# Expert gates of the first 128 tokens: from one-hot products on TensorE to indexed stores into a table in HBM

## The chip, the cores and the metric

The kernel runs on one core of a Trainium2 chip. The metric is the device time of one execution in microseconds (us). The engines are named as in the profile: PE is TensorE's matmuls, PEld its weight loads, DVE is VectorE, ACT is ScalarE, POOL is GpSimd, SP is SyncE, which issues the DMAs of the kernel before.

## What is computed

Two transformer blocks over 256 tokens. The change lies in the feed-forward layer of the first one, a retrieval over 16,384 single-neuron experts. Each of 8 heads picks 16 experts of a token by two half keys, and the gates are a softmax over the picked scores. Cut to what matters:

```python
def peer_ffn(n, w_q, sub_keys, expert_u, expert_v):
    q = (t @ w_q).reshape(T, 8, 2, 128)
    s = jnp.einsum('thsd,hskd->thsk', q, sub_keys)
    v_half, i_half = lax.top_k(s, 16)
    cand = (v_half[:, :, 0, :, None] + v_half[:, :, 1, None, :]).reshape(T, 8, 256)
    best, pos = lax.top_k(cand, 16)
    i1 = jnp.take_along_axis(i_half[:, :, 0], pos // 16, axis=-1)
    i2 = jnp.take_along_axis(i_half[:, :, 1], pos % 16, axis=-1)
    experts = (i1 * 128 + i2).reshape(T, 128)
    gates = jax.nn.softmax(best, axis=-1).reshape(T, 128)
    act = jax.nn.gelu(jnp.einsum('td,tkd->tk', x, expert_u[experts])) * gates
    return jnp.einsum('tk,tkd->td', act, expert_v[experts])
```

Two heads may pick the same expert for a token; their gates then add up.

## The kernel before, in words

The kernel does not gather experts. It computes the activations of all 16,384 experts for all 256 tokens, multiplies them with a dense matrix of gates that is zero where an expert was not picked, and multiplies the result with all of `expert_v`. Every weight comes in chunks of 512 KB. SP loads a chunk into `raw` (`pump_dma`, L345, four buffers), ACT copies it into a rounded high part `wh` and DVE subtracts to get the low part `wl` (`pump_split`, L352, three buffers of each), and PE multiplies with three products per pair of parts.

The stages around the change stand in this order. The mixer reads 45 chunks of `w_in` (L949). Then come 16 of `w_out`, 16 of `w_q`, which give the scores, then 128 chunks of `expert_u` (the loop at L1223, two chunks for each `j2`), which I call the U stage, and 128 chunks of `expert_v`, the V stage. A U chunk is 24 matmuls of 128x256 (`wa`, L436); chunk j holds the 128 experts with i2 = j, the partition is i1. Its result of two chunks lies in one PSUM bank `acc`, and `u_post` (L1206) puts the gelu of it into `hact`, a table in SBUF of 128 partitions x 128 chunks x 256 tokens (tiles `hactA`, `hactB`). In the V stage `w_split` (L1237) splits two chunks of `hact` into `wth` (ACT) and `wtl` (DVE), and `v_mm` multiplies.

Beside the chunks run side jobs: Python generators that are advanced by so many units after each chunk (`tick`, L412), which sets where their instructions stand in the program. A scheduler then places the instructions of all engines; each engine runs its own in order. `peer_side` (L1163) is the side job of the gates. For each block `tb` of 128 tokens, `topk1` picks 16 of each half, `topk2` combines them and ends with `isel` (minus i1, and i2) and the gates `gt`. PE transposes these into `idxT`. `g_side` (L1111) then takes four tokens at a time, which I call a quartet: ACT makes a one-hot matrix of i1 in `oA` (four instructions and one more over all four), DVE makes one of i2 scaled by the gates in `oB` (four instructions), and PE multiplies them into a bank `sm`, the dense gates of the token:

```python
act(oA[:, j], iota, AF.Square, bias=idxT[:, 0, t:t + 1])
ts(oB[:, j], iota, idxT[:, 1, t:t + 1], idxT[:, 2, t:t + 1], OP.is_equal, OP.mult)
...
mm(pg[:, j], A_[:, j], B_[:, j], True, True)
```

DVE multiplies the gates into those chunks of `hact` that are there already; ACT copies the gates of the later chunks into `hact`, where `u_post` multiplies the gelu onto them. In the kernel before, the first block's quartets are given out in turn with the selection of the second block (`alternate`, L1149), and the second block's quartets come after both.

Of the kernel before, what the change touches and what calls it, by code (L numbers as in the profile page):

```python
# [38 lines left out]
def _consts():  # L39
    cols, off = [], 0  # L40

    def put(name, arr):
        nonlocal off
        arr = np.asarray(arr, np.float32).reshape(128, -1)
        _C[name] = (off, arr.shape[1])
        cols.append(arr)
        off += arr.shape[1]

    i = np.arange(128)
    put("ident", np.eye(128))  # L50
    put("iota", np.broadcast_to(i[None, :], (128, 128)))
    first = off
# [155 lines left out]
def build(tc, a, out):  # L208
    nc = tc.nc
    top = ExitStack()  # L210
    with top:
# [53 lines left out]

        V, S, PE, SP = nc.vector, nc.scalar, nc.tensor, nc.sync

        def mm(o, l, r, start, stop_):
            PE.matmul(o, l, r, start=start, stop=stop_)  # L269

        def bank(tag):
            return ps.tile([128, 512], F, name=tag, tag=tag, bufs=4 if tag == "acc" else 2)
# [68 lines left out]
        st = {"n": 0, "dma": 0, "split": 0, "done": 0}  # L341
        RAW, SA, HB = 4, 2, 3
        raws, hs, ls, spare = {}, {}, {}, {}

# [390 lines left out]

        B0, B1 = slice(T0, T0 + 128), slice(T0 + 128, T0 + 256)

        def ssd_group(g):
            cc = slice(g * 384, (g + 1) * 384)
            hh = slice(6 * g, 6 * g + 6)  # L740
# [179 lines left out]
        def sc_chunks(i):  # L920
# [23 lines left out]
            post(1, fn)  # L944
            post(2, lambda ac=ac, i=i: tt(mixl[:, 12 + i], ac, mixh[:, 12 + i].bitcast(F), OP.subtract))

        z_chunk()
        si = 0
        for what in MIX[1:]:  # L949
# [52 lines left out]
        idxT = tp.tile([128, 3, 256], F, name="idxT")  # L1002
        ust = {"J": 0, "T": 0, "sc": set(), "topk": -1}

        scores = Pool(112, 128).tile([128, 32, 128], F, name="scores")

# [39 lines left out]
        def topk2(tb):  # L1046
# [18 lines left out]
                    top16(best[:, h], pos[:, h], cd[:, h, :50], w[:, :50], part)  # L1065
                yield 0.7

            gt = tp.tile([128, 8, 16], F, name="gt")
# [19 lines left out]
            tt(gt, gt, gs_[:, :, None].to_broadcast([128, 8, 16]), OP.mult)  # L1088
            yield
            isel = ih.bitcast(F).rearrange("p (s h) r -> p s h r", s=2)  # L1090
            for s in range(2):
                for h2 in range(4):
                    eq = gp.tile([128, 8, 64], F, name="cdw", bufs=1)
                    eq = eq.rearrange("p h c -> p (h c)").rearrange("p (h k r) -> p h k r", h=2, k=16)
                    hh = slice(2 * h2, 2 * h2 + 2)
                    tt(eq, iota[:, None, None, :16].to_broadcast([128, 2, 16, 16]),
                       pf[:, s, hh, :, None].to_broadcast([128, 2, 16, 16]), OP.is_equal)
                    yield 0.6
                    tt(eq, eq, ir[:, hh, s, None, :].to_broadcast([128, 2, 16, 16]), OP.mult)
                    yield 0.6  # L1100

                    V.tensor_reduce(out=isel[:, s, hh], in_=eq, op=OP.add, axis=AX.X, negate=(s == 0))
                    yield 0.6
            pt = bank("tr")
            for j, src in enumerate((isel[:, 0], isel[:, 1], gt)):
                PE.transpose(pt[:, j * 128:(j + 1) * 128], src.rearrange("p h r -> p (h r)"), ident)
            yield
            V.tensor_copy(idxT[:, :, tb * 128:(tb + 1) * 128],  # L1108
                          pt[:, :384].rearrange("p (j t) -> p j t", j=3))

        def g_side(tb):  # L1111
            ab, pm = None, None
            for t4 in range(tb * 32, tb * 32 + 34):
                if pm is not None:
                    q4, pg = pm
                    J = ust["J"]
                    tsl = (q4 * 4, q4 * 4 + 4)
                    for jj, _, hv_ in Hact(0, J, *tsl):
                        hv_ = hv_.rearrange("p j t -> p t j")
                        tt(hv_, pg[:, :, jj], hv_, OP.mult)  # L1120
                    ust["T"] = q4 * 4 + 4
                    late = (pg, J, tsl)
                    pm = None
                else:
                    late = None
                if ab is not None:
                    q4, A_, B_ = ab
                    pg = bank("sm").rearrange("p (t j) -> p t j", t=4)
                    for j in range(4):
                        mm(pg[:, j], A_[:, j], B_[:, j], True, True)  # L1130
                    pm = (q4, pg)
                    ab = None
                if t4 < tb * 32 + 32:
                    oA = gp.tile([128, 4, 128], F, name="oA", bufs=2)
                    oB = gp.tile([128, 4, 128], F, name="oB", bufs=2)

                    for j in range(4):
                        t = t4 * 4 + j
                        act(oA[:, j], iota, AF.Square, bias=idxT[:, 0, t:t + 1])
# [9 lines left out]
        def alternate(g1, g2):  # L1149
            gens = [g1, g2]  # L1150
            while gens:
                for g in list(gens):
                    try:
                        c = next(g)
                        yield c
                    except StopIteration:
                        gens.remove(g)
# [5 lines left out]
        def peer_side():  # L1163
            yield from paced(topk1(0), 1.3)
            yield from paced(topk2(0), 1.3)

            def second():
                yield from topk1(1)
                yield from topk2(1)

            yield from paced(alternate(g_side(0), second()), 1.4)
            yield from paced(g_side(1), 1.6)

        skp = Pool(0, 16, 8)

# [29 lines left out]

        def u_post(j2, pp):  # L1206
            def f1():
                T = ust["T"]
                if T > 0:
                    act(pp[:, :, :T], pp[:, :, :T], AF.Gelu)  # L1210

                    def f2():
                        for _, tsl, hv_ in Hact(2 * j2, 2 * j2 + 2, 0, T):
                            tt(hv_, pp[:, :, tsl], hv_, OP.mult)

                    post(1, f2)
                for _, tsl, hv_ in Hact(2 * j2, 2 * j2 + 2, T, 256):
                    act(hv_, pp[:, :, T + tsl.start:T + tsl.stop], AF.Gelu)
                ust["J"] = 2 * j2 + 2

            post(1, f1)

        for j2 in range(64):  # L1223
            if j2 == 46:
                while ust["topk"] < 1:
                    step_sides()
            pp = bank("acc").rearrange("p (j t) -> p j t", j=2)
            for j in range(2):
                wa(pp[:, j], xTh, xTl, T0, 256)
            u_post(j2, pp)  # L1230
        drain()
        wp = Pool(128, 136, 2)
        spare[333] = Pool(136, AREA)
        pacc = [bank("acc") for _ in range(4)]
        wts = {}

        def w_split(j2):  # L1237
            wth = wp.tile([128, 2, 256], FR, name="wth")
            wtl = wp.tile([128, 2, 256], FR, name="wtl")
            for _, tsl, hv_ in Hact(2 * j2, 2 * j2 + 2, 0, 256):  # L1240
                act(wth[:, :, tsl], hv_, AF.Copy)
                tt(wtl[:, :, tsl], hv_, wth[:, :, tsl].bitcast(F), OP.subtract)
            wts[j2] = (wth, wtl)
# [473 lines left out]
```

## Time and profile before

| what | value |
|---|---|
| median of 3 runs | 1701.99 us (1701.15 to 1703.01) |
| the profiled execution's own time | 1703.75 us |
| its span, first to last instruction | 1702.0 us |
| granted TensorE clock over the span | 0.999 |
| DMA traffic | 289.78 MB, mean 170 GB/s |

The span leaves out 1.75 us around the first and the last instruction. The profile's first part gives the busy time of each engine; windows of the trace give the same for one stage; the timeline gives the instructions in order. Since every engine works in order, an instruction that waits holds back what stands behind it on its own engine.

### The profile page before, as it was taken

Reading aid. Unit: us, or ns where it says so; the run is one execution under the profiler, and the core shown is the slowest. Engines: PE = TensorE matmul, PEld = TensorE weight load, DVE = VectorE, ACT = ScalarE, POOL = GpSimd, SP = SyncE. Lnnn points to the kernel's source line nnn. Section 1 sums busy time; section 2 is a strip of 40 time slices with the busy share of each in tenths; the row PEclk is TensorE's granted clock in tenths of the full one; section 3 lists DMA queues with packets and bytes.
Section 4 is the critical chain, followed back from the end, with each engine's and each line's share of the span. In section 5 each row is a group of like instructions: output and inputs, shape, how many; then the busy total and the mean of one; then the engine's idle time right before and its main releaser. Section 6 shows DMA issues by size and latency. Waiting matters only on the chain. (4 is left out here: it accounts for less than half of the span.)

```text
span 1702.0 us, 29712 instructions
## 1 busy us (share of the span) xinstructions
PE 1680.4 (99%) x11373; PEld 1530.6 (90%) x11373; DVE 1270.7 (75%) x2531; ACT 1020.1 (60%) x1792; POOL 0.2 (0%) x4
## 2 busy tenths in 40 slices
PE   8999999999999999999999999999999999999998
PEld 6999889999999999988888888898899988899986
DVE  6789778989985599855555565897787757887754
ACT  5877456567985698644444455733565544765543
POOL 0000000000000000000000000000000000000000
PEclk9999999999999999999999999999999999999999
DMA  6444565554455554555555595544566665356663
GB/s 210 137 136 125 156 214 166 171 176 137 141 155 184 167 150 145 156 182 189 191 187 186 188 312 189 183 125 139 159 196 187 185 184 169 103 160 186 186 184 114
DMA packets 82113, 289.78 MB, mean 170 GB/s; under 512 B 9250, under 2 KB 11810, under 8 KB 81715
## 3 DMA queue, kind: packets, MB, share of 16 engines
q1 hardware_dynamic: 81970, 287.89, 54.5%
q8 instruction: 89, 1.46, 0.3%
q14 instruction: 54, 0.43, 0.1%
HBM read 285.75 MB, written 2.10 MB: 169 GB/s over the span
## 5 line engine op out<-in xcount | busy, mean ns | idle before, releaser
L275 DVE TENSOR_TENSOR wl<-raw,wh 128x1024 fp32r<-128x1024 f32 x523 | 638.7, 1222 | 293.4 <-ACT wh L287 290.7
L287 ACT ACTIVATE wh<-raw 128x1024 fp32r<-128x1024 f32 x523 | 551.8, 1057 | 425.5 <-PE acc L269 397.4
L269 PE MATMUL acc<-xTh,wh 128*128 128x256 f32 (+2 forms) x2184 | 543.5, 287 | 0.2 <-ACT xTh L287 0.2
L269 PE MATMUL acc<-xTl,wh 128*128 128x256 f32 (+2 forms) x2184 | 533.5, 282 | 1.0 <-DVE xTl L275 1.0
L269 PEld LDWEIGHTS acc<-xTl,wh 128*128 128x128 f32 x2184 | 412.8, 189 | 2.2 <-DVE xTl L275 1.2
L269 PEld LDWEIGHTS acc<-xTh,wh 128*128 128x128 f32 x2184 | 411.9, 189 | 3.2 <-issue 1.7
L269 PE MATMUL acc<-xTh,wl 128*128 128x256 f32 (+2 forms) x2184 | 305.7, 282 | 0.0
L269 PEld LDWEIGHTS acc<-xTh,wl 128*128 128x128 f32 x2184 | 279.4, 189 | 0.0
L269 PE MATMUL acc<-wh,wth 128*128 128x512 f32 x512 | 204.0, 399 | 0.0
L269 PE MATMUL acc<-wl,wth 128*128 128x512 f32 x512 | 200.8, 392 | 0.0
L269 PE MATMUL acc<-wh,wtl 128*128 128x512 f32 x512 | 162.5, 395 | 0.0
L269 PEld LDWEIGHTS acc<-wh,wth 128*128 128x128 f32 x512 | 96.1, 188 | 25.2 <-issue 0.3
L269 PEld LDWEIGHTS acc<-wh,wtl 128*128 128x128 f32 x512 | 96.2, 188 | 23.2
L269 PEld LDWEIGHTS acc<-wl,wth 128*128 128x128 f32 x512 | 96.2, 188 | 21.4
L287 ACT ACTIVATE oA<-cst,idxT 128x128 f32<-128x128 f32 x256 | 83.9, 393 | 3.5 <-DVE idxT L1108 2.8
L269 PE MATMUL sm<-oB,oA 128*128 128x128 f32 x512 | 68.4, 277 | 4.4 <-ACT hactB L287 3.7
L281 DVE TENSOR_SCALAR oB<-cst,idxT 128x128 f32<-128x128 f32 x256 | 71.6, 343 | 1.0 <-PE sm L269 0.9
L269 PE MATMUL acc<-wl,fh 128*128 128x512 f32 x176 | 69.6, 396 | 0.0
L269 PE MATMUL acc<-wh,fl 128*128 128x512 f32 x176 | 69.6, 396 | 0.0
L269 PE MATMUL acc<-wh,fh 128*128 128x512 f32 x176 | 69.6, 395 | 0.0
L269 PEld LDWEIGHTS sm<-oB,oA 128*128 128x128 f32 x512 | 62.6, 192 | 6.0 <-ACT hactB L287 5.6
L287 ACT ACTIVATE wth<-hactA 128x512 fp32r<-128x512 f32 x48 | 30.4, 633 | 60.6 <-PE acc L269 58.3
(319 smaller groups left out, 2087.6 us busy)
## 6 DMA issues: line engine op xcount, KB each, us to landing
raw<-in_u SPq DMA_DIRECT2D x128, 512.0 KB, 3.6
raw<-in_v SPq DMA_DIRECT2D x128, 512.0 KB, 3.5
raw<-in_up SPq DMA_DIRECT2D x88, 512.0 KB, 3.6
raw<-in_w_in SPq DMA_DIRECT2D x45, 512.0 KB, 3.6
raw<-in_dn SPq DMA_DIRECT2D x44, 512.0 KB, 3.6
raw<-in_hg_in SPq DMA_DIRECT2D x32, 512.0 KB, 3.6
raw<-in_w_out SPq DMA_DIRECT2D x16, 512.0 KB, 3.6
raw<-in_w_q SPq DMA_DIRECT2D x16, 512.0 KB, 3.6
```

The lines of the kernel that those rows point to most:

```text
L269: PE.matmul(o, l, r, start=start, stop=stop_)
L275: V.tensor_tensor(out=o, in0=x, in1=y, op=op)
L281: V.tensor_scalar(o, x, s1, s2, op0=op0, op1=op1)
L287: S.activation(o, i, f, **kw)
```

## The change

The second block's tokens keep their quartets. For the first 128 tokens no one-hot matrix and no product is made. Their gates go through a table of 128 x 128 x 128 numbers in HBM, `gtab`, in which element i1 x 16384 + i2 x 128 + token holds the gate.

- In the mixer stage a new side job `zero_side` writes zeros over the table: 16 DMAs of 512 KB on SP's queue, from one tile of zeros.
- In the selection of the first block the loops over the four pairs of heads and the two halves are exchanged, so that a pair of heads is finished at a time. After each pair DVE computes the 32 places (`gpart`, `gplace`), and `scatter` issues 16 indexed DMAs for each head on POOL: each adds 128 numbers of 4 bytes, one for each token, at 128 places of the table. The DMAs of one head are declared to hit different places; each head waits for all of the head before it, because two heads may hit one place.
- `u_post` writes the gelu of the first block's tokens plainly into `hact`.
- `g_load` reads two chunks of the table (128 KB, 1 KB for each partition) on SP's queue into one of two buffers `gts`. The first two reads stand beside `j2 == 61` in the U stage; the others two `j2` ahead in `w_split`. Each read waits for the last head's stores. An order-only tie puts a read behind the matmul that was the last one written.
- In `w_split` DVE multiplies the table's two chunks into `hact` before the split.
- `peer_side` no longer alternates: selection of block 0, selection of block 1, quartets of block 1, at other rates.

```diff
+        gtab = dram.tile([128 * 128 * 128, 1], F, name="gtab")
+        gtv = gtab.rearrange("(a c) o -> a (c o)", a=128)
+        zero = m2.tile([128, 256], F, name="zero", bufs=1)
+        V.memset(zero, 0.0)
+        def zero_side():
+            for i in range(16):
+                yield
+                SP.dma_start(gtv[:, i * 1024:(i + 1) * 1024].rearrange("a (k c) -> a k c", k=4),
+                             zero[:, None, :].to_broadcast([128, 4, 256]))
...
+        add_side(zero_side(), 0.5)
...
-            for s in range(2):
-                for h2 in range(4):
+            for h2 in range(4):
+                for s in range(2):
...
+                if tb == 0:
+                    flat = lambda t: t.rearrange("p h r -> p (h r)")
+                    pl, gp_ = (t[:, 32 * h2:32 * h2 + 32] for t in (gpart, gplace))
+                    ts(pl, flat(isel[:, 0, hh]), -16384.0, C("row"), OP.mult, OP.add)
+                    stt(gp_, flat(isel[:, 1, hh]), 128.0, pl, OP.mult, OP.add)
+                    scatter(2 * h2)
+                    scatter(2 * h2 + 1)
+            if tb == 0:
+                return
...
+        def scatter(h):
+            before, head = list(last), []
+            for r in range(16):
+                c = slice(h * 16 + r, h * 16 + r + 1)
+                ins = nc.gpsimd.indirect_dma_start(
+                    out=gtab, out_offset=bass.IndirectOffsetOnAxis(ap=gplace[:, c].bitcast(U32), axis=0),
+                    in_=gval[:, h, r:r + 1], in_offset=None, compute_op=OP.add)
+                for other in head:
+                    tc.declare_no_dep(ins.ins, other.ins, reason="other places")
+                after(ins, before)
+                head.append(ins)
+            last[:] = head
...
-            yield from paced(alternate(g_side(0), second()), 1.4)
-            yield from paced(g_side(1), 1.6)
+            yield from paced(topk1(1), 1.1)
+            yield from paced(topk2(1), 1.1)
+            yield from paced(g_side(1), 1.25)
...
+        def g_load(j2):
+            gts[j2] = gtp.tile([128, 2, 128], F, name="gts")
+            ins = SP.dma_start(gts[j2].rearrange("p j t -> p (j t)"), gtv[:, j2 * 256:(j2 + 1) * 256])
+            after(ins, last)
+            tc.add_manual_dep(ins.ins, st["mm"].ins.name, mybir.DependencyInfo(
+                mybir.DependencyClass.NoSync, mybir.DependencyReason.SCHED_ONLY), reason="order")
         for j2 in range(64):
+            if j2 == 61:
+                g_load(0)
+                g_load(1)
...
+            g = gts.pop(j2)
+            for _, tsl, hv_ in Hact(2 * j2, 2 * j2 + 2, 0, 128):
+                tt(hv_, hv_, g, OP.mult)
+            if j2 + 2 < 64:
+                g_load(j2 + 2)
```

The order of the built programs shows the moves. On PE, in the first third of the U stage, this is a stretch before:

```order
L269 MATMUL acc<-xTl,wh 128x256
L269 MATMUL acc<-xTh,wl 128x256 x8
L269 MATMUL sm<-oB,oA 128x128 x4
L269 MATMUL acc<-xTh,wh 128x256
L269 MATMUL acc<-xTl,wh 128x256
```

and this is the same stretch now:

```order
L272 MATMUL acc<-xTl,wh 128x256
L272 MATMUL acc<-xTh,wl 128x256 x8
L272 MATMUL acc<-xTh,wh 128x256
L272 MATMUL acc<-xTl,wh 128x256
L272 MATMUL acc<-xTh,wh 128x256
```

A quartet (`sm<-oB,oA`, four products) is gone between two chunks. 32 of the 64 quartets of the program are gone in this way, those that stood behind 27 to 68 chunks of U. The other 32 stood behind 91 to 123 chunks and stand behind 66 to 104 now. Besides, one group of three transposes has moved with the second block and another is gone.

On POOL nothing but four memsets stood before. Now the first of the 128 stores stand there so (the names `DMASW` are the eight semaphores that these DMAs signal when they have landed, `DMAHW` those of SP's DMAs):

```order
L1763 MEMSET const-uint8-127 128x1
L1770 UNCONDITIONAL_BRANCH [waits barrier_Pool_Activation_PE_DVE_SP_gather]
L1150 DMA gtab<-gval,gplace 2097152x1 [waits DMAHW4_49,DMAHW3_49,DMAHW5_49,DMAHW2_49,DMAHW6_49,DMAHW1_49,DMAHW7_49,DMAHW0_49,DVE_49]
L1150 DMA gtab<-gval,gplace 2097152x1 x7
L1150 DMA gtab<-gval,gplace 2097152x1 [waits DMASW0_49]
L1150 DMA gtab<-gval,gplace 2097152x1 [waits DMASW1_49]
L1150 DMA gtab<-gval,gplace 2097152x1 [waits DMASW2_49]
```

Up to eight stores are under way at once, the ninth waits for the first, the tenth for the second and so on, and the first store of each further head waits for all eight semaphores.

On SP, at the seam from U to V, the loads stood so before:

```order
L348 DMA raw<-in_u 128x1024 [waits DMAHW2_49,DVE_49]
L348 DMA raw<-in_u 128x1024 [waits DMAHW3_49,DVE_49]
L348 DMA raw<-in_v 128x1024 [waits DMAHW4_49,DVE_49]
L348 DMA raw<-in_v 128x1024 [waits DMAHW5_49,DVE_49]
L348 DMA raw<-in_v 128x1024 [waits DMAHW6_49,DVE_49]
```

and now:

```order
L350 DMA raw<-in_u 128x1024 [waits DMAHW3_49,DVE_49]
L1266 DMA gts<-gtab 128x256 [waits DMASW4_49,DMASW3_49,DMASW5_49,DMASW2_49,DMASW6_49,DMASW1_49,DMASW7_49,DMASW0_49,PE_49]
L1266 DMA gts<-gtab 128x256
L350 DMA raw<-in_v 128x1024 [waits DMAHW4_49,DVE_49]
L350 DMA raw<-in_v 128x1024 [waits DMAHW5_49,DVE_49]
```

The first read of the table waits for the last stores and stands ahead of the first load of `expert_v`; further on, one read stands behind every two loads.

## Rows read from the trace of the kernel before

**Rows 1.** The page's first part: engine, busy us, share of the span, instructions.
```profile
PE 1680.4 (99%) x11373; PEld 1530.6 (90%) x11373; DVE 1270.7 (75%) x2531; ACT 1020.1 (60%) x1792; POOL 0.2 (0%) x4
```

**Rows 2.** Busy time by windows: mixer, scores, first quartets, second quartets, V stage.
```profile
core 0: us, PE busy (x) PEld busy (x) DVE busy (x) ACT busy (x) POOL busy (x), PEclk, DMA share, GB/s
27.00:100.00 73.00, 72.96 (x494) 66.52 (x493) 55.83 (x117) 56.20 (x99) 0.00 (x0) 1.00 0.49 153
230.00:270.00 40.00, 39.96 (x311) 38.34 (x310) 33.63 (x90) 23.92 (x45) 0.00 (x0) 1.00 0.69 215
365.00:475.00 110.00, 105.88 (x897) 104.75 (x896) 108.67 (x382) 94.78 (x218) 0.00 (x0) 1.00 0.46 139
584.00:719.70 135.70, 135.67 (x1165) 135.46 (x1164) 124.57 (x260) 115.74 (x272) 0.00 (x0) 1.00 0.49 147
719.70:1060.00 340.30, 340.30 (x1461) 273.82 (x1460) 193.56 (x205) 164.87 (x200) 0.00 (x0) 1.00 0.62 203
```

**Rows 3.** Timeline of PE, two quartets with one chunk between: start us, us, instruction, count.
```profile
689.82 1.05 PE L269 MATMUL sm<-oB,oA 128*128 128x128 f32 x8
690.63 0.36 PE L269 MATMUL acc<-xTh,wh 128*128 128x256 f32 x1
...
693.54 1.05 PE L269 MATMUL sm<-oB,oA 128*128 128x128 f32 x8
694.35 0.36 PE L269 MATMUL acc<-xTh,wh 128*128 128x256 f32 x1
```

**Rows 4.** Timeline of SP's queue, U stage before the first quartet, the loads merged.
```profile
303.82 73.85 SPq L348 DMA_DIRECT2D raw<-in_u  x26
```

**Rows 5.** The products of `oB` and `oA`, and PE's waits before them.
```profile
L269 PE MATMUL sm<-oB,oA x512: 272/275/378, 369.7 to 705.5; 128*128 128x128 f32 x171
PE sm L269 <- ACT hactB L287: 3.7, 5, 2.0
PE sm L269 <- DVE oB L281: 0.7, 1, 0.7
```

**Rows 6.** Timeline of PE: first matmul of the U stage and of the V stage.
```profile
291.68 0.36 PE L269 MATMUL acc<-xTh,wh 128*128 128x256 f32 x1
719.78 0.39 PE L269 MATMUL acc<-wh,wth 128*128 128x512 f32 x1
```

**Rows 7.** DVE, groups by form in the U stage: busy us, mean ns of one.
```profile
L275 DVE TENSOR_TENSOR wl<-raw,wh 128x1024 fp32r<-128x1024 f32 x128 | 156.1, 1220 | 54.5 <-ACT wh L287 54.5
L281 DVE TENSOR_SCALAR oB<-cst,idxT 128x128 f32<-128x128 f32 x256 | 71.6, 343 | 1.0 <-PE sm L269 0.9
L275 DVE TENSOR_TENSOR hactB<-acc,hactB 128x256 f32<-128x256 f32 x17 | 6.9, 418 | 0.0
```

**Rows 8.** The tile `wth` and the copy into `wh`: ns min/median/max, or mean.
```profile
L287 ACT ACTIVATE wth<-hactA x48: 624/633/635, 708.0 to 977.2; 128x512 fp32r<-128x512 f32 x48
L275 DVE TENSOR_TENSOR wtl<-hactA,wth x48: 686/695/695, 708.6 to 977.9; 128x512 fp32r<-128x512 f32 x48
L287 ACT ACTIVATE wh<-raw 128x1024 fp32r<-128x1024 f32 x523 | 551.8, 1057 | 425.5 <-PE acc L269 397.4
```

**Rows 9.** Timeline of DVE: second and eighth reduction of the first block's selection.
```profile
328.27 0.68 DVE L1102 TENSOR_REDUCE ih<-cdw 128x32 f32<-128x512 f32 x1
...
349.40 0.67 DVE L1102 TENSOR_REDUCE ih<-cdw 128x32 f32<-128x512 f32 x1
```

**Rows 10.** DMA issues: count, KB each, median us from issue to landing.
```profile
raw<-in_u SPq DMA_DIRECT2D x128, 512.0 KB, 3.6
qs<-in_sk SPq DMA_DIRECT2D x16, 64.0 KB, 3.3
out_dram<-zo SPq DMA_DIRECT2D x4, 256.0 KB, 2.3
```

**Rows 11.** SP's loads of the sub keys and of `expert_v`: ns of one issue, first and last start.
```profile
L1178 SPq DMA_DIRECT2D qs<-in_sk x16: 327/400/1415, 240.4 to 272.0; - x16
L348 SPq DMA_DIRECT2D raw<-in_v x128: 327/328/328, 703.2 to 1061.2; - x128
```

More of the change, by code (lines that the diff above doesn't have):

```diff
@@ L51, in _consts @@
     put("iota", np.broadcast_to(i[None, :], (128, 128)))
+    put("row", i[:, None])
     first = off
@@ L266, in build @@
         V, S, PE, SP = nc.vector, nc.scalar, nc.tensor, nc.sync
+        st = {"n": 0, "dma": 0, "split": 0, "done": 0}
         def mm(o, l, r, start, stop_):
-            PE.matmul(o, l, r, start=start, stop=stop_)
+            st["mm"] = PE.matmul(o, l, r, start=start, stop=stop_)
         def bank(tag):
@@ L340, in build @@
             srcs += [a[n][i] for i in range(cnt)]
-        st = {"n": 0, "dma": 0, "split": 0, "done": 0}
         RAW, SA, HB = 4, 2, 3
@@ L1001, in build @@
         ihf = tp.tile([128, 16, 16], F, name="ihf")
-        idxT = tp.tile([128, 3, 256], F, name="idxT")
-        ust = {"J": 0, "T": 0, "sc": set(), "topk": -1}
+        idxT = tp.tile([128, 3, 128], F, name="idxT")
+        gplace = tp.tile([128, 128], I32, name="gplace")
+        gpart = tp.tile([128, 128], F, name="gpart")
+        gval = tp.tile([128, 8, 16], F, name="gval")
+        ust = {"J": 0, "T": 128, "sc": set(), "topk": -1}
         scores = Pool(112, 128).tile([128, 32, 128], F, name="scores")
@@ L1066, in topk2 @@
                 yield 0.7
-            gt = tp.tile([128, 8, 16], F, name="gt")
+            gt = gval if tb == 0 else tp.tile([128, 8, 16], F, name="gt")
             tt(gt, best, best[:, :, 0:1].to_broadcast([128, 8, 16]), OP.subtract)
@@ L1107, in topk2, with after @@
             yield
-            V.tensor_copy(idxT[:, :, tb * 128:(tb + 1) * 128],
-                          pt[:, :384].rearrange("p (j t) -> p j t", j=3))
+            V.tensor_copy(idxT, pt[:, :384].rearrange("p (j t) -> p j t", j=3))
+        last = []
+        def after(ins, others):
+            for other in others:
+                tc.add_manual_dep(ins.ins, other.ins.name, mybir.DependencyInfo(
+                    mybir.DependencyClass.Sync, mybir.DependencyReason.DATA), reason="the same places")
+        def scatter(h):
[10 more added lines that the diff above has]
+            last[:] = head
         def g_side(tb):
@@ L1138, in g_side @@
                         t = t4 * 4 + j
+                        t -= tb * 128
                         act(oA[:, j], iota, AF.Square, bias=idxT[:, 0, t:t + 1])
@@ L1147, in g_side @@
                 yield 1.2 + 0.004 * ust["J"]
[L1149 to L1157, printed above, removed]
         def paced(gen, rate):
@@ L1165, in peer_side @@
             yield from paced(topk2(0), 1.3)
-            def second():
-                yield from topk1(1)
-                yield from topk2(1)
-            yield from paced(alternate(g_side(0), second()), 1.4)
-            yield from paced(g_side(1), 1.6)
+            yield from paced(topk1(1), 1.1)
+            yield from paced(topk2(1), 1.1)
+            yield from paced(g_side(1), 1.25)
         skp = Pool(0, 16, 8)
@@ L1208, in f1 @@
                 T = ust["T"]
-                if T > 0:
-                    act(pp[:, :, :T], pp[:, :, :T], AF.Gelu)
+                if T > 128:
+                    act(pp[:, :, 128:T], pp[:, :, 128:T], AF.Gelu)
                     def f2():
-                        for _, tsl, hv_ in Hact(2 * j2, 2 * j2 + 2, 0, T):
-                            tt(hv_, pp[:, :, tsl], hv_, OP.mult)
+                        for _, tsl, hv_ in Hact(2 * j2, 2 * j2 + 2, 128, T):
+                            tt(hv_, pp[:, :, 128 + tsl.start:128 + tsl.stop], hv_, OP.mult)
                     post(1, f2)
-                for _, tsl, hv_ in Hact(2 * j2, 2 * j2 + 2, T, 256):
-                    act(hv_, pp[:, :, T + tsl.start:T + tsl.stop], AF.Gelu)
+                for t0, t1 in ((0, 256),) if T == 128 else ((0, 128), (T, 256)):
+                    for _, tsl, hv_ in Hact(2 * j2, 2 * j2 + 2, t0, t1):
+                        act(hv_, pp[:, :, t0 + tsl.start:t0 + tsl.stop], AF.Gelu)
                 ust["J"] = 2 * j2 + 2
             post(1, f1)
+        gtp = Pool(144, AREA, 2)
+        gts = {}
+        def g_load(j2):
[4 more added lines that the diff above has]
+                mybir.DependencyClass.NoSync, mybir.DependencyReason.SCHED_ONLY), reason="order")
         for j2 in range(64):
+            if j2 == 61:
+                g_load(0)
+                g_load(1)
             if j2 == 46:
@@ L1232, in build @@
         wp = Pool(128, 136, 2)
-        spare[333] = Pool(136, AREA)
+        spare[333] = Pool(136, 144)
         pacc = [bank("acc") for _ in range(4)]
```

## The prediction

> **What bounds the kernel now.** I read the page's first part first: PE is busy 99% of the span [rows 1], so the time falls only where PE gets less to do, and rises only where something makes PE wait. POOL has four instructions in all [rows 1]; it is a free queue. Then the windows by stage [rows 2]. Two stretches carry the products of one-hot matrices, the first quartets at 365 to 475 and the second at 584 to 719.7. In both DVE is nearly as full as PE: 108.67 of 110 us and 124.57 of 135.7 us. In the first, PE loses 4.1 us (105.88 of 110); in the second almost nothing. [...] Then the timeline, for what a quartet costs PE [rows 3], and the places where PE waited for one [rows 5].
>
> **The change part by part.** The sum is made against the profiled execution: 1703.75 us, of which 1702.0 is the span. The median of the three runs, 1701.99, is 1.76 us below it, and I take that off at the end.
>
> Products removed. From the chunk after one quartet to the chunk after the next is 694.35 - 690.63 = 3.72 us [rows 3]. Without quartets, 26 loads and so 26 chunks take 73.85 us, 2.84 each [rows 4]. A quartet so costs PE 0.88 us, although the records of its eight matmuls alone span 1.05 us, since their ends overlap with the next chunk. All 256 tokens have 512 records [rows 5], 64 quartets. The whole U stage agrees: 719.78 - 291.68 = 428.1 us [rows 6], and 128 x 2.84 + 64 x 0.88 = 419.8, plus the waits and a few small products. 32 quartets go: **-28.2 us**. A group of three transposes goes too, 0.3 us by the same kind of row: **-0.3 us**.
>
> Waits removed. PE waited 3.7 + 0.7 = 4.4 us for `hactB` and `oB` before such products [rows 5]. The first stretch's window lacks 4.1 us of PE, so nearly all belongs to the quartets that go [rows 2]: **-4.1 us**.
>
> Selection and second quartets moved. The selection of block 1 used to share DVE with the first quartets. The 32 span 41 chunks, by the prices above 41 x 2.84 + 32 x 0.88 = 145 us from 369.7 on [rows 5], so some 23 lie in the window of 110 us. Their `oB` alone was 23 x 4 x 0.343 = 32 us of DVE [rows 7]; DVE keeps some 77 us in a stretch that shrinks by 23 x 0.88 + 4.1 = 24 us, to 86. No wait follows from that; the bound is the 4.1 us that this stretch lost before. The second quartets now come 32 to 38 chunks instead of 32 to 32, and end 24 chunks before the U stage does. At the denser spacing PE lost nothing [rows 2]: **0**, and there is no tail to drain.
>
> Multiplication in the V stage. Each of 64 pairs gets one more DVE instruction of 256 columns, 0.418 us by the nearest form [rows 7], 26.8 us. DVE is busy 193.56 of 340.3 us there [rows 2], so it rises to about 65%. Its cover is that spare time: **0**. If the cover were gone, all 26.8 us would show.
>
> Reads of the table. 64 DMAs of 128 KB. A load of 512 KB lands after 3.6 us and one of 64 KB after 3.3 [rows 10]; one issue holds SP 0.33 us [rows 11]. They are issued two `j2` ahead, four chunks, more than 10 us before their use: **0**. SP's own place is the seam: the first read stands ahead of the first load of `expert_v`, so if it waits, all loads behind it wait.
>
> Zeros. 16 writes of 512 KB in packets of 1 KB enter SP's queue beside the loads of the mixer. A 4-KB packet costs an engine 0.20 us: 0.62 x 16 engines over 203 GB/s [rows 2]. By their bytes the writes so hold each engine 26 us; if a 1-KB packet cost as much as a 4-KB one, 102 us. The loads use 0.49 of the engines there [rows 2], which leaves 45 us of the some 88 us in which the writes stand. The nearest row decides: 15 of the 16 loads of 64 KB, in packets of 512 B, lie in the window at 230 to 270 [rows 11], and its share of 0.69 at 215 GB/s is only 0.033 above the V stage's rate; that is 21 us of one engine for 1,920 packets, 11 ns a packet above the price of its bytes. So 26 + 6 = 32 us, hidden: **0**, the bounds being 0 and +57.
>
> Indexed stores. This is the unknown: 128 DMAs of 128 numbers each, with an addition in HBM, issued by POOL. No row shows one. They must be through before the table is read. The first pair of heads can start when the second reduction ends, 328.27 + 0.68 = 328.95, and two small DVE operations later, about 329.4; the last pair's places are there at 350.1 [rows 9]. Every later store stands behind the earlier ones, so 128 stores follow on 329.4. On the other side, the V stage starts at 719.8 - 32.6 = 687.2. Behind the first read lies either 3.6 + 0.42 + 0.63 + 0.69 = 5.3 us (landing, product, `wth`, `wtl`) or, for the held-up load, 3.6 + 1.06 + 1.22 = 5.9 [rows 7, 8, 10]. So the stores may last until 681.3, that is **2.75 us each** on the mean. Up to eight are under way at once. From below: 0.33 us per issue [rows 11] plus eight gaps of 3.3 us between heads, 0.54 us each. From above: one after the other at the landing of the smallest load, 3.3 us each [rows 10]. The write of `out` lands after 2.3 us [rows 10], and even 2.3 in single file would do. With eight under way I take about half of the upper end, 1.7 us, so that they end near 547, 134 us early: **0**. [...]
>
> Sum: -28.2 - 0.3 - 4.1 = **-32.6 us**. 1703.75 - 32.6 = 1671.2 for such an execution, **1669.4** for the median, some 1664 to 1677 with the small bounds (no removed wait comes back, or it does and a few us of seam are added).
>
> **The rivals.** *Late table (slower).* The stores go in single file at 3.3 us: POOL writes 128 addresses for each, and nothing in the trace says that this overlaps. They end at 329.4 + 422.4 = 751.8, 70.5 us after 681.3. SP holds the table's read and all loads of `expert_v` behind it, PE stands still at the seam, and the time is 1669.4 + 70.5 = 1740. It costs from 2.75 us per store on, and at 3.0 us (32.6 / 128 more) it eats the gain. For it speaks that DVE, whose operations read and write SBUF beside POOL, is nearly full in that stretch [rows 2]; against it, eight stores under way and 350 us of time. I give it 0.13, and 0.05 to the part between 2.75 and 3.0, 1677 to 1700. [...]
>
> *Full DMA engines.* 16,384 tiny stores compete with the loads. At the price of a 4-KB packet they hold each engine 205 us; from 329 to 681 the loads leave about 0.4 of 352 us, 141. Loads or stores are then 64 us late, 1733. At 11 ns each above their bytes they hold an engine 11 us and nothing shows. [...] 0.05.
>
> *Zeros in the way.* The upper price of a packet holds: the mixer's loads come 57 us late, 1726. The same row speaks against it: 0.02.
>
> *No change.* DVE, near its limit in both stretches, holds PE up by what was saved, as it did by 4.1 us before, or several small waits together do: within 3.4 us of 1702, 0.05.
>
> **How the numbers follow.** The forecast has 0.70, the partly late table 0.05, late table 0.13, full engines 0.05, zeros 0.02, no change 0.05. About 0.2%, 3.4 us, is what a measurement of this kernel can tell from no change. Faster: 0.70 + 0.05 and a little of the last case, 0.76; same 0.04; slower 0.20. The predicted median is 1669. The range reaches from 1663 to 1695: it holds the forecast's own 1664 to 1677 and most of the partly late table, and with the tails of the forecast about 0.75 to 0.8 of the chances; the slower cases lie outside.
>
> **What would show it.** Right: 256 records of `sm<-oB,oA` instead of 512; V's first matmul near 687; the last store tens of us before the read of `gts`, and SP's first read waiting for nothing; PE busy throughout the V stage. Wrong: PE idle at the seam with SP's read released by POOL's DMAs; PE waiting for `wh` between 330 and 680 with loads landing much later than 3.6 us; or such waits in the mixer, beside the zeros.

## The result, and the profile after

The changed kernel takes **1679.9 us** (four runs, 1678.8 to 1680.9) where the kernel before takes 1702.1: a ratio of 0.987 with an interval of 0.9853 to 0.9887. It is 22.2 us faster; 32.6 were forecast, so the direction is right and a third of the gain is missing. The time lies inside the range of 1663 to 1695, but above the 1664 to 1677 that the forecast's own sum gave. (Four later runs of the same kernel, the tenth experiment, spread from 1670.6 to 1680.1; the spread is taken up there.) The profiled execution took 1680.89 us, its span 1679.1.

The page's first part, beside [rows 1]:

```profile
PE 1657.2 (99%) x11114; PEld 1498.8 (89%) x11114; DVE 1219.5 (73%) x2388; ACT 949.6 (57%) x1590; POOL 242.6 (14%) x132
```

Its part on the DMA queues, the row of the indexed stores (packets, MB, share of 16 engines' span):

```profile
q0 software_dynamic: 18432, 0.07, 2.7%
```

PE has 23.2 us less to do and is still busy 99%. POOL now works 242.6 us. Next the windows by stage, beside [rows 2]; the last one has the length of the V window there:

```profile
27.00:100.00 73.00, 72.95 (x498) 66.64 (x498) 56.48 (x119) 56.33 (x99) 0.00 (x0) 1.00 0.79 253
365.00:475.00 110.00, 108.19 (x891) 106.02 (x891) 82.81 (x214) 51.10 (x60) 86.10 (x43) 1.00 0.75 187
688.50:1028.80 340.30, 337.43 (x1425) 264.67 (x1424) 199.54 (x257) 160.80 (x195) 0.00 (x0) 1.00 0.67 221
```

In the mixer the zeros raise the DMA share from 0.49 to 0.79 and PE loses nothing. From 365 to 475 PE lacks 1.8 us instead of 4.1. In the V stage it now lacks 2.9, where it lacked nothing. That number is smaller than the loss, as the starts of V's products will show. First the products of `oB` and `oA`, beside [rows 5]:

```profile
L272 PE MATMUL sm<-oB,oA x256: 273/275/275, 484.3 to 620.2; 128*128 128x128 f32 x128
```

Half of them are gone. PE's timeline where U and V begin, beside [rows 6]:

```profile
290.67 0.36 PE L272 MATMUL acc<-xTh,wh 128*128 128x256 f32 x1
688.51 0.40 PE L272 MATMUL acc<-wh,wth 128*128 128x512 f32 x1
```

U begins 1.0 us earlier and V at 688.5 instead of 719.8: **31.3 us are won by then**, 1.3 fewer than forecast. V's products, before and then now (ns of one, first and last start):

```profile
L269 PE MATMUL acc<-wh,wth x512: 392/399/477, 719.8 to 1078.5; 128*128 128x512 f32 x171
L272 PE MATMUL acc<-wh,wth x512: 387/393/479, 688.5 to 1055.7; 128*128 128x512 f32 x171
```

They took 358.7 us and now take 367.2: **8.5 us are given back in V**, and from there to the end the kernels take 623.5 and 623.4 us. PE's busy time hides a part of it: the mean of a matmul with `wl` rose from 392 to 402 ns, so the 512 of them count 205.7 us of busy time where they counted 200.8. That they wait for their operand in this time is my reading.

The waits of the V stage (engine and line, what it waited for: us in total, times, longest), DVE's main one before and then those of now:

```profile
DVE wl L275 <- ACT wh L287: 115.2, 123, 2.2
DVE hactA L278 <- DMA gts<-gtab: 114.0, 46, 3.2
DVE hactB L278 <- DMA gts<-gtab: 24.9, 15, 3.6
PEld acc L272 <- DVE wl L278: 16.7, 41, 1.1
PE acc L272 <- DVE wl L278: 2.8, 6, 0.8
```

Before, DVE waited there for `wh` from ACT, and PE for no operand. Now DVE waits for the table's reads in 61 of 64 pairs, 2.3 us each, and PE for `wl`. The DMA issues (count, KB each, median us to landing), beside [rows 10], the loads of `expert_v` before and then those of now:

```profile
raw<-in_v SPq DMA_DIRECT2D x128, 512.0 KB, 3.5
raw<-in_u SPq DMA_DIRECT2D x128, 512.0 KB, 3.7
raw<-in_v SPq DMA_DIRECT2D x128, 512.0 KB, 4.4
gtab<-zero SPq DMA_DIRECT2D x16, 512.0 KB, 6.7
gts<-gtab SPq DMA_DIRECT2D x64, 128.0 KB, 3.8
gtab<-gval,gplace POOLq DMA_INDIRECT x128, 4.2
```

And the two queues in the middle of the V stage, DVE's and then SP's:

```profile
801.27 0.42 DVE L278 TENSOR_TENSOR hactA<-hactA,gts 128x256 f32<-128x256 f32 x1 [2.31 <-DMA gts<-gtab]
801.61 2.35 DVE L278 TENSOR_TENSOR wl<-raw,wh 128x1024 fp32r<-128x1024 f32 x2
803.89 0.69 DVE L278 TENSOR_TENSOR wtl<-hactA,wth 128x512 fp32r<-128x512 f32 x1
807.03 0.43 DVE L278 TENSOR_TENSOR hactA<-hactA,gts 128x256 f32<-128x256 f32 x1 [2.46 <-DMA gts<-gtab]
...
802.86 0.33 SPq L350 DMA_DIRECT2D raw<-in_v  x1
803.24 0.42 SPq L1266 DMA_DIRECT2D gts<-gtab  x1
```

Read them as one circle. The product starts at 801.27. Behind it in DVE's order stand two `wl`; the first ends near 802.8 and frees a buffer of `raw`, so SP's load goes out at 802.86. The table's read stands behind that load and goes out at 803.24. It is there for the next product at 807.03, 3.8 us later. The circle is 1.97 us plus the landing, 5.76 us here, and a pair takes PE 5.60. The circle is longer, so it sets the pace, and both `wl` come late for PE; 8.5 us over 62 pairs are 0.14 each.

### The profile page after: what moved, and what is told of

Same layout as the page of the kernel before. It is cut to its first block, busy times and chain, and to the rows that moved or that the text cites. A ratio compares the mean times of both kernels' runs of the same rounds, so it can differ in the third digit from the quotient of the medians.

```text
span 1679.1 us, 29135 instructions
## 1 busy us (share of the span) xinstructions
PE 1657.2 (99%) x11114; PEld 1498.8 (89%) x11114; DVE 1219.5 (73%) x2388; ACT 949.6 (57%) x1590; POOL 242.6 (14%) x132
## 3 DMA queue, kind: packets, MB, share of 16 engines
q0 software_dynamic: 18432, 0.07, 2.7%
## 5 line engine op out<-in xcount | busy, mean ns | idle before, releaser
L1150 POOL DMA_INDIRECT gtab<-gval,gplace x128 | 242.4, 1893 | 389.1 <-DVE gplace L287 328.5
L272 PE MATMUL acc<-wl,wth 128*128 128x512 f32 x512 | 205.7, 402 | 3.0 <-DVE wl L278 2.8
L278 DVE TENSOR_TENSOR hactA<-hactA,gts 128x256 f32<-128x256 f32 x48 | 20.3, 426 | 117.0 <-DMA gts<-gtab 117.0
L272 PE MATMUL acc<-wh,xTh 128*128 128x512 f32 x112 | 47.1, 421 | 0.7 <-ACT wh L290 0.7
L272 PE MATMUL acc<-wl,xTh 128*128 128x512 f32 x112 | 45.0, 403 | 0.5 <-DVE wl L278 0.5
```

What stands on the lines that cost most here:

```text
L272: st["mm"] = PE.matmul(o, l, r, start=start, stop=stop_)
L278: V.tensor_tensor(out=o, in0=x, in1=y, op=op)
L1150: ins = nc.gpsimd.indirect_dma_start(out=gtab, out_offset=bass.IndirectOffsetOnAxis(ap=gplace[:, c].bitcast(U32), axis=0), in_=gval[:, h, ...
```

## The experiments

Two rivals stood against this reading: (A) the 64 products are simply too much for DVE, (B) the reads' traffic disturbs the loads of `expert_v`, which land after 4.4 us instead of 3.5.

**First: the product later.** The product is tied in order to the end of the last chunk written; all work and traffic stay.

```diff
+        ends = []
...
-                tt(hv_, hv_, g, OP.mult)
+                ins = V.tensor_tensor(out=hv_, in0=hv_, in1=g, op=OP.mult)
+                if len(ends) >= 1:
+                    tc.add_manual_dep(ins.ins, ends[-1].ins.name, mybir.DependencyInfo(
+                        mybir.DependencyClass.NoSync, mybir.DependencyReason.SCHED_ONLY), reason="order")
...
                 v_mm(j, hl, t)
+            ends.append(st["mm"])
```

> All the work and all the traffic of the changed kernel stay. Only the place of the product hact*gts in VectorE's order moves: it is tied in order to the end of the chunk that has just been emitted, so it stands one `wl` later, and its read gets a chunk's time (2.8 us) more to land. Theory (the product stands directly behind its read in VectorE's order, waits 2.3 us for it, and the two `wl` behind it come late for TensorE): VectorE's wait for `gts` goes from 139 us to near 0, TensorE no longer waits for `wl`, the V stage takes 358.7 us from its first to its last `wth` product as before the change, not 367.2, and the time is 1679.9 - 8.5 = 1671.4 (1670 to 1673). Rival A (the 64 products themselves, 64 x 0.42 = 27 us of VectorE, are too much for its queue): nothing goes, 1679.9 within 2. Rival B (64 reads of 128 KB disturb the loads of `expert_v`, which land after 4.4 us instead of 3.5): nothing goes, 1679.9 within 2.

Measured: **1671.5 us** (1671.3 to 1672.3), ratio 0.9824 (0.9808 to 0.9841), below the interval of the changed kernel's first four runs; the tenth experiment puts that in doubt for the times, not for the length of the V stage. V's products take 357.4 us:

```profile
L272 PE MATMUL acc<-wh,wth x512: 390/393/499, 688.8 to 1046.2; 128*128 128x512 f32 x171
```

Its timeline of DVE:

```profile
801.73 1.23 DVE L278 TENSOR_TENSOR wl<-raw,wh 128x1024 fp32r<-128x1024 f32 x1 [0.96 <-ACT wh L290]
802.87 0.42 DVE L1296 TENSOR_TENSOR hactA<-hactA,gts 128x256 f32<-128x256 f32 x1
804.51 1.23 DVE L278 TENSOR_TENSOR wl<-raw,wh 128x1024 fp32r<-128x1024 f32 x1 [1.23 <-ACT wh L290]
```

Its one wait for `gts`, that of the first product, still in U:

```profile
DVE hactA L1296 <- DMA gts<-gtab: 1.9, 1, 1.9
```

The window 756 to 1028 in the changed kernel:

```profile
756.00:1028.00 272.00, 269.13 (x1134) 210.21 (x1133) 161.37 (x211) 128.96 (x158) 0.00 (x0) 1.00 0.69 225
```

And in this one:

```profile
756.00:1028.00 272.00, 272.00 (x1172) 220.51 (x1171) 168.98 (x217) 134.08 (x163) 0.00 (x0) 1.00 0.70 231
```

In V the product waits for nothing, and both rivals fall, since product and traffic are all still there: in the sixth experiment, which has the product at the same place, the loads of `expert_v` still land after 4.3 us, and V's products take 358.0. One detail of the expectation was wrong: counted in the orders, the product stands three `wl` later, not one. From a read's issue to its product it is now 10.6 us, where it was 3.8.

**Second and third: reads alone, product alone.** The one leaves out the products, the other the reads (the factor is then `ones`, and the product is tied as in the first).

```diff
-            for _, tsl, hv_ in Hact(2 * j2, 2 * j2 + 2, 0, 128):
-                tt(hv_, hv_, g, OP.mult)
```

```diff
-            g = gts.pop(j2)
+            g = ones[:, None, :].to_broadcast([128, 2, 128])
...
-            if j2 + 2 < 64:
-                g_load(j2 + 2)
```

> Leaves out the products hact*gts in the V stage, so the outputs lack the gates of the first 128 tokens; the 64 reads of the table are still issued at their places. Theory (the wait of the product holds up `wl`): without it the V stage takes 358.7 us, the time is 1671.4 (1670 to 1673). Rival A (the products' own time on VectorE): also 1671.4. Rival B (traffic of the reads): 1679.9 within 2, with loads of `expert_v` landing after 4.4 us.

> Leaves out the 64 reads of the table and multiplies by ones instead, so the outputs lack the gates of the first 128 tokens; the products stand where the first experiment has them. Theory (only the wait costs): V stage 358.7 us, time 1671.4 (1670 to 1673). Rival A (the products' own time on VectorE): 1679.9 within 2. Rival B (traffic of the reads): 1671.4.

Measured: 1672.2 us (1670.3 to 1675.4) and 1672.3 (1671.6 to 1675.0); V's products take 357.1 and 357.4 us. Neither part costs V anything by itself; the product without reads in its old place was not run. The times agree less well than the stages: in the profiled execution of the reads alone (1675.4 us) DVE stood 9.0 us before its first `wtl` until the stores were through, and V began at 693.3. That comes of the edit and not of the circle.

**Fourth: no stores.** The calls of `scatter` are left out.

```diff
-                    scatter(2 * h2)
-                    scatter(2 * h2 + 1)
```

> Leaves out the 128 indexed stores, so the table holds zeros and the outputs lack the experts of the first 128 tokens; reads and products stay. Theory (the stores are hidden beside TensorE's work; the last one ends some 40 us before the first read): the V stage begins at 688.5 as in the changed kernel, within 1.5, and the time is 1679.9 within 2. Rival (128 stores of 128 numbers hold up loads or VectorE in the U stage): V begins up to 1.3 us or more earlier, time 1678 or less; and if the wait for the reads is theirs, the V stage shortens too.

Measured: 1676.9 us, V's first matmul at 688.3. The start of V says that the stores are hidden. The time is inconclusive: the four runs lie between 1673.1 and 1680.8. In the profiled one the product waited 1.1 to 1.7 us in each pair from 701 to 770, and some 2.5 after that. The tenth experiment takes up this spread.

**Fifth: the reads earlier.** They are tied two chunks earlier, the product to nothing.

```diff
...
-            tc.add_manual_dep(ins.ins, st["mm"].ins.name, mybir.DependencyInfo(
+            tie = ends[-3] if len(ends) >= 3 else st["mm"]
+            tc.add_manual_dep(ins.ins, tie.ins.name, mybir.DependencyInfo(
```

> The changed kernel with its reads tied two chunks (one pair, 5.7 us) earlier; the product is tied to nothing, as in the changed kernel. Theory (the product follows its read: the scheduler puts it directly behind it in VectorE's order, two `wl` ahead of its `wtl`): the product comes one pair earlier as well, waits for its read as before (some 139 us in all), and nothing is won: 1679.9 within 2. Rival (the read stands too late in SyncE's queue, whatever the product does): the wait goes, 1671.5.

Measured: 1681.6 us, 0.9884 (0.9867 to 0.99). As expected, the product came along by a pair in DVE's order, and DVE's wait stayed (the waits of the V stage):

```profile
DVE hactA L278 <- DMA gts<-gtab: 112.6, 45, 3.9
```

**Sixth and ninth: the stores of all heads together.** On the first experiment. The sixth writes all stores behind the loop over the pairs; the ninth also exchanges the loops back, so that the places themselves come later.

```diff
-                    scatter(2 * h2)
-                    scatter(2 * h2 + 1)
             if tb == 0:
+                for h in range(8):
+                    scatter(h)
                 return
```

```diff
-            for h2 in range(4):
-                for s in range(2):
+            for s in range(2):
+                for h2 in range(4):
...
+            for h2 in range(4 if tb == 0 else 0):
...
```

> On the first experiment (1671.5), with one part of the change undone: all stores begin when the places of all eight heads are there, not two heads at a time. Theory: the stores begin near 350 instead of 329 and take as long, so the last begins near 650 instead of 629, still some 20 us ahead of the first read: 1671.5 within 1.5. Rival (the early beginning is needed, as a late table or as spread load): SyncE's first read waits for a store, V begins later, 1675 or more.

> On the first experiment (1671.5): the selection goes by sides again (first sides of all four pairs of heads, then second sides), as before the change, so no pair's places are there before the fifth of eight reductions. In the sixth experiment the stores still began at 329.8, since only their data hold them, not the place where they are written; this edit moves the data. Theory: the first store starts some 10 to 20 us later, at 339 to 350, the last ends near 642 to 653, still ahead of the first read near 671: 1671.5 within 1.5. Rival (the early beginning is needed): SyncE's first read waits, V begins later, over 1675.

Measured: 1671.5 and 1670.6 us. The sixth moved nothing: the stores still began at 329.8, for POOL waits for data, not for the place where a store is written. In the ninth they ran from 341.0 to 637.8 and the first read went out at 671.1, without a wait. Beginning two heads at a time is worth nothing here: it moves the first store by 12 us and the last by 8, within a margin that is there anyway.

**Seventh: the price of a late table.** On the first experiment, with the stores in groups of four that wait for each other.

```diff
                 head.append(ins)
-            last[:] = head
+                if r % 4 == 3:
+                    before, head = head, []
+            last[:] = before
```

> On the first experiment (1671.5), with the stores in 32 groups of four, each group waiting until the one before has landed, instead of 8 groups of sixteen. It prices the late table. At a boundary GpSimd sat idle 3.1 us instead of 0.3; 24 boundaries more make 24 x 2.8 = 67 us, so the last store begins near 629 + 67 = 696 and lands near 701. By the prediction's rule the reads must start 5.9 us ahead of V, at 688.5 - 5.9 = 682.6; so V comes 701 - 682.6 = 18 us late: 1690 (1680 to 1700), with SyncE's first read released by a store and TensorE idle at the seam. Rival (the table is not needed so early, or stores overlap anyhow): 1671.5.

Measured: 1697.2 us (1692.0 to 1699.7). The last store began at 699.2, and 28 waits for landings took 91.6 us, 3.3 each. In its timeline SP's first read, and the matmul before which PE stood still:

```profile
702.25 0.80 SPq L1268 DMA_DIRECT2D gts<-gtab  x2
705.89 2.07 PE L272 MATMUL acc<-xTh,wl 128*128 128x256 f32 x8 [23.46 <-DVE wl L278]
```

And the window in which it stood:

```profile
670.00:702.00 32.00, 12.43 (x105) 12.22 (x104) 2.14 (x3) 2.78 (x4) 20.57 (x13) 0.75 0.25 26
```

V began at 714.4, 25.6 us late where 18 were expected. The mechanism is the prediction's rival of the late table; its limit was drawn too late. PE stood still in U (`xTh` is U's operand), not at the seam: the first product stands in DVE's order ahead of `wl` of U's last chunks. The stop is 23.46 us. The other 2.2 are the granted clock, which fell while PE stood: it was 0.50 from 702 to 706, where the windows of the changed kernel above show 1.00, and PE's next matmuls of 128x256 show 0.41 us until 709.7 and 0.28 from 710.1 on, as before the stop. A read that landed as fast as this one (2.0 us from issue to product) must so be out by 702.25 - 23.46 = 678.8. In the first experiment the first product followed its read after 4.1 us and in the changed kernel after 5.2, and with these it is 676.7 and 675.6, not 681.3.

**Eighth: the reads untied.** The changed kernel without `tc.add_manual_dep` in `g_load`.

> The changed kernel without the tie of the reads to products. The scheduler then puts the first read ahead of load 111 of `expert_u`, and two reads before nearly every load after it. Theory: SyncE stops at the first read, near 620, until the last store has landed near 635, so loads come some 8 us late; then each load stands behind two reads whose buffers wait for VectorE's products and these for landings (3.8 us), some 5.7 us per load instead of 2.84 for about 29 loads, +83 us; the V stage, without reads, is 8.5 us shorter: about 1762 (1720 to 1800). Rival (the tie does nothing, for the reads need only be early): 1671 to 1680.

Measured: 1692.2 us. Direction right, size far off: the tie is worth 12 us against the changed kernel's 1679.9, 18 against the tenth experiment's 1674.05, not 80. SP's timeline:

```profile
631.24 0.33 SPq L1266 DMA_DIRECT2D gts<-gtab  x1
631.66 0.38 SPq L350 DMA_DIRECT2D raw<-in_u  x1
632.09 1.95 SPq L1266 DMA_DIRECT2D gts<-gtab  x2
634.85 0.33 SPq L350 DMA_DIRECT2D raw<-in_u  x1
```

The window behind the last read:

```profile
756.00:1028.00 272.00, 272.00 (x1167) 218.82 (x1166) 155.57 (x163) 132.03 (x159) 0.00 (x0) 1.00 0.62 208
```

SP stopped at the first read until 631.2, but a load with its two reads then took 3.2 us, not 5.7: the two reads overlap and land after 2.9. V began at 702.1, 13.6 us late. Some 10 us more went in V's first 55, while reads still stood before nearly every load: V's products take 367.7 us in all, one of them waited 4.6 us for `hactB`, and the granted clock was 0.94 on the mean from 700 to 757. The last read went out at 746.9, and from 756 on PE is full: V without the circle runs at its old pace.

**Tenth: the changed kernel once more**, on the chip of the ninth and eleventh. **Eleventh: the product tied to `ends[-2]`**, a chunk earlier than in the first.

> The changed kernel once more, on the same chip as the others of this call. Theory: 1679.9 within 1.5.

> The first experiment with the product tied one chunk earlier still (the end of the chunk before last). The order on VectorE in the V stage is the same (one `wl`, the product, the second `wl`, then `wtl`), so theory: 1671.5 within 1.5, no wait for `gts`. Rival (the place of the product has to be hit to one chunk, for the lead of the read shrinks by 2.8 us): 1675 or more.

Measured: 1674.05 us for the tenth, its four runs 1670.6, 1673.5, 1674.6 and 1680.1; a miss. The eleventh 1670.8 (1670.6 to 1671.6), with 7.9 us from read to product. In the tenth's profiled execution, the slowest, DVE's products begin thus:

```profile
729.92 0.43 DVE L278 TENSOR_TENSOR hactA<-hactA,gts 128x256 f32<-128x256 f32 x1 [1.01 <-DMA gts<-gtab]
735.64 0.43 DVE L278 TENSOR_TENSOR hactA<-hactA,gts 128x256 f32<-128x256 f32 x1 [1.15 <-DMA gts<-gtab]
741.21 0.42 DVE L278 TENSOR_TENSOR hactA<-hactA,gts 128x256 f32<-128x256 f32 x1 [1.14 <-DMA gts<-gtab]
...
804.12 0.43 DVE L278 TENSOR_TENSOR hactA<-hactA,gts 128x256 f32<-128x256 f32 x1 [2.56 <-DMA gts<-gtab]
810.32 0.43 DVE L278 TENSOR_TENSOR hactA<-hactA,gts 128x256 f32<-128x256 f32 x1 [2.90 <-DMA gts<-gtab]
```

From 702 to 769 a period is 5.60 us on the mean, PE's own pace; from 775 to 928 it is 5.89, and V's products take 366.1 us in all. The break-even landing is 5.60 - 1.97 = 3.63 us, and the reads of the changed kernel landed after 3.8 on the median, 3.5 at the least. In the first window of the fourth experiment (690 to 760), where the wait was 1.3 on the mean, the median was 3.6. So the circle stands at its break-even, and the changed kernel has no one time. That its faster executions are those in which reads land a little earlier fits this, but they left no trace, so it is not shown. The four versions with the product later and the table read keep within 1.6 us each. What makes the landings of one execution shorter than another's stays open.

**Twelfth: a longer circle.** DVE's and SP's orders are held as in the changed kernel by ties, with one more operation of DVE behind the product.

```diff
...
+        def prod(j2):
+            g = gts.pop(j2)
+            for _, tsl, hv_ in Hact(2 * j2, 2 * j2 + 2, 0, 128):
+                tt(hv_, hv_, g, OP.mult)
+                st["prod"] = V.tensor_tensor(out=hv_, in0=hv_, in1=ones[:, None, :].to_broadcast([128, 2, 128]), op=OP.mult)
...
```

> The changed kernel with the orders of its VectorE and SyncE in the V stage held as they were (the product, two `wl`, `wtl`; read behind the load before it), and one more VectorE operation of 256 columns per pair directly behind the product, a multiplication by ones, so the outputs stay. Theory (a closed loop: product, first `wl`, load that needs the freed buffer, read behind it in SyncE's queue, landing, next product; 2.0 us + landing per pair, where TensorE takes 5.60): the operation makes the loop 0.34 us longer, 5.9 to 6.1 with landings of 3.6 to 3.8, so every pair is late from the first on: V stage some 61 x 0.4 = 24 us longer than without the loop, 1671 + 24 = 1695 (1688 to 1704), and no run near 1671. Rival (no loop; VectorE is 60% busy there and can take 64 x 0.42 = 27 us): as the changed kernel, 1671 to 1681.

Measured: 1721.5 us (1717.6 to 1722.3), ratio 1.0118 (1.0102 to 1.0135): **slower than the kernel before**, with one operation of 0.42 us more per pair on an engine that was 59% busy there.

```profile
803.49 0.43 DVE L278 TENSOR_TENSOR hactA<-hactA,gts 128x256 f32<-128x256 f32 x1 [2.16 <-DMA gts<-gtab]
803.95 0.43 DVE L1298 TENSOR_TENSOR hactA<-hactA,ones 128x256 f32<-128x256 f32 x1
804.29 2.36 DVE L365 TENSOR_TENSOR wl<-raw,wh 128x1024 fp32r<-128x1024 f32 x2
809.68 0.43 DVE L278 TENSOR_TENSOR hactA<-hactA,gts 128x256 f32<-128x256 f32 x1 [2.42 <-DMA gts<-gtab]
...
805.96 0.43 SPq L1270 DMA_DIRECT2D gts<-gtab  x1
```

From product to read (805.96) it is now 2.47 us, so the circle is 6.2 on the mean to 929, and 6.6 behind it, where the later loads of that stage (`hold`, gains) stand in SP's queue too. The rival falls: DVE's free time was of no use to work that lay on the circle. I had expected 24 us and got 50. The operation needs the product's result and starts 0.46 us after it, where the first `wl` starts 0.34 us after the operation; so it adds 0.46 to 0.5 us and not 0.34, and I had left out the later loads. The ties alone, without the operation, were not run; that the operation is the cause rests on the 0.5 us by which the way from product to read grew, and on the period.

The version of the first experiment beats both kernels, by 30 us and by 3 to 8.

## Why the prediction was right, and where it was not

*Products, transposes and waits removed, -32.6.* Right to about a microsecond: V began at 688.5, forecast 687.2. U itself shrank from 428.1 to 397.8 us, 30.3 instead of 32.6: of the 4.1 us of waits only 2.3 went. The start of U 1.0 us earlier, which was not forecast, gave part of that back. With the product moved, the whole is 1671.5, and the sum said 1669.4.

*Selection and second quartets moved, 0.* Right: PE is busy in all of 475 to 688.5.

*Multiplication, 0.* Right by itself (third experiment). The forecast of 65% for DVE (59% were measured) missed that DVE, in order, was late while it had time: it waited 2.3 us for the table in 61 of 64 pairs.

*Reads of the table: "issued two `j2` ahead, four chunks, more than 10 us before their use: 0".* **This is the step that failed.** It was read from the code, where the read is written two pairs ahead. The scheduler orders DVE's queue by itself and put the product ahead of its place in the code, two `wl` before the `wtl` that needs it. That it goes by the time at which it takes the read to have landed fits the fifth experiment, where the product moved along with the read, but is not shown. Measured: 3.8 us from issue to product, and 8.5 us lost in the profiled execution; by their times none to 10 in others. The prediction's own sign, PE busy throughout the V stage, did not come. The prediction named the seam between SP's read and SP's loads, but only for the first read; the same seam repeats in every pair, and the order of DVE, which could be seen beforehand, shows it.

*Zeros, 0.* Right: U begins 1.0 us earlier; loads beside the zeros landed after 4.5 us on the median from 27 to 100, before 3.6.

*Stores, 1.7 us each.* Inside the bounds of 0.54 and 3.3, too low: 128 starts from 329.0 to 629.3 are 2.36 us apart. They ended some 40 us ahead of the first read, which waited for nothing, so 0 was right. The limit of 2.75 us each becomes 2.70 to 2.73 by the seventh experiment, with 675.6 to 678.8 in place of 681.3. *Full DMA engines* did not happen: 18,432 packets took 2.7% of 1679.1 us, 45 us of each engine, 39 ns a packet, between my 11 and 200; the loads of `expert_u` land after 3.7 us, before 3.6. One store took 1.54 us of POOL at the least and 1.89 on the mean, and only some were held up (below); issue to landing took 4.2 on the median. Within a head the next store started 0.30 us after the end of the one before on POOL (0.81 once).

*The range.* It holds the result by luck. It was drawn up to 1695 for a partly late table, and the stores were some 40 us early; what took the time beyond the sum's own 1664 to 1677 is the circle, which had no term.

## What to carry to other kernels

How far ahead a load ran was decided here by the orders of the queues that issue and use it, not by where it is written: 3.8 us from issue to product in the changed kernel and 10.6 in the first experiment, with the read written at the same place (no run here changed the number of buffers). So subtract the issue from the use in the trace, or count what stands between them. Look for circles: a use that delays something which frees a buffer for a load that stands ahead of the next read. Such a circle cost about its whole excess over PE's period in each turn once it was longer (5.76 against 5.60 us in the pair read above, 0.14 a pair lost on the mean), whatever the shares of busy time said, and it was opened by moving one member alone; moving read and use together changed nothing here.

## What the runs showed of the hardware

An indexed store on POOL was held up by DVE's `wl`, an operation with both inputs in SBUF: 2.22 us on the mean for the stores that start beside one, 1.61 for the others. The changed kernel, POOL and then DVE:

```profile
616.22 2.52 POOL L1150 DMA_INDIRECT gtab<-gval,gplace  x1 [0.30 <-issue]
619.05 1.54 POOL L1150 DMA_INDIRECT gtab<-gval,gplace  x1 [0.30 <-issue]
...
616.09 1.23 DVE L278 TENSOR_TENSOR wl<-raw,wh 128x1024 fp32r<-128x1024 f32 x1 [1.20 <-ACT wh L290]
617.23 1.06 DVE L278 TENSOR_TENSOR hactA<-sm,hactA 128x384 f32<-128x384 f32 x1
619.81 1.23 DVE L278 TENSOR_TENSOR wl<-raw,wh 128x1024 fp32r<-128x1024 f32 x1 [1.43 <-ACT wh L290]
```

The first store starts 0.13 us into a `wl` and ends 1.42 us after it; the second starts before one and takes 1.54. Of the 128, the 59 that start while a `wl` runs take 2.22 us on the mean, most of them until 1.42 us after its end; the other 69 take 1.61, half of them 1.55 or less. The 14 that start beside `hactA<-sm,hactA`, with one input in PSUM, took 1.56 and the 15 beside `oB` 1.58. Nor is it `wl` alone: the store at 421.73 us also ended 1.42 us after the end of a product of the selection, `cdw<-cst,vh`, with both inputs in SBUF. DVE itself was not slowed: a `wl` beside stores takes 1.22 us on the mean, as before [rows 7].
